# Window and retention scores two heads at a time, modulation chunks in pairs

## The chip, the core and the metric

The kernel runs on one core of a Trainium2 chip. The metric is the time of one execution on the device, in microseconds (us). TensorE is called PE here, its weight loads PEld, VectorE DVE, ScalarE ACT, GpSimd POOL and SyncE SP.

## What is computed

One inference step of a two-layer diffusion transformer, for 128 context tokens (block 0) and 256 latent tokens (blocks 1 and 2) of 1024 elements. Layer 0 mixes by retention (8 heads) beside banded attention (8 query heads, 2 key heads, 64 elements each); layer 1 by differential attention beside a Fourier transform; each layer ends in a SwiGLU network. Shift, scale and gate of each layer come from a conditioning vector. What matters here, cut from the reference:

```python
mod = jax.nn.silu(cond) @ w_mod[l] + b_mod[l]
sh1, sc1, g1, sh2, sc2, g2 = jnp.split(mod[:, None, :], 6, axis=-1)
u = layer_norm(x) * (1.0 + sc1) + sh1
...
band = jnp.abs(a - b + Q_BLOCK) <= WINDOW
s = jnp.einsum('bqhgd,bkhd->bhgqk', q, k).astype(f32) * (q.shape[-1] ** -0.5)
s = jnp.where(mask, s, -jnp.inf)
p = jax.nn.softmax(jnp.concatenate([s, sink_col], -1), axis=-1)[..., :-1]
return jnp.einsum('bhgqk,bkhd->bqhgd', p.astype(v.dtype), v)
...
att = jnp.einsum('bhid,bhjd->bhij', qc, kc) * intra
o = jnp.einsum('bhij,bhjv->bhiv', att, vc) + jnp.einsum('bhid,bhdv->bhiv', qc, s) * q_decay[..., None]
```

## The kernel before

Python code names every instruction; a scheduler puts those of each engine into one order by priority and by its own estimate of when they are ready, and each engine's queue then runs in that order. `hmm` (L116) issues a product with raised priority. Tiles come from pools with a fixed number of buffers: a new tile of a name's tag waits until an old one has been read for the last time.

Large weights are read as 512 KB units into `raw` tiles (`raw_unit`, L157, five buffers), and `split` (L167) makes two tiles of each, the rounded value (ACT, a cast into tag `wr`) and the remainder (DVE, a subtraction into tag `wl`); each tag has five buffers (`NWR`, L41). A `raw` buffer is free after the split. A block of 128 tokens against a slab of 512 columns is 24 products of 512 columns, 3 per 128 rows of the model dimension (`in_block`, L366), into a bank of PSUM from `bankA` (L82), of which there are two.

The stretch of the change is `mixer_ab`, layer 0. Its steps stand in `AORDER` (L33): a letter and a number each, in the order in which the code issues them. `Q`, `G` load the slabs `rqk` and `rvg` of a half of the retention heads (half 0 is heads 0 to 3, half 1 heads 4 to 7), `R`, `V` multiply them, `W` advances the window, `C` does the retention of a half (`ret_core`, L1037), `N` its norm, `M` one modulation vector of layer 0 (2 the gate, 3 the shift, 4 the scale), `E` loads the units `wo` of the output projection. The loads are issued by SP in program order.

The window goes head by head: `win1` (L846) makes the scores `ws` of one head (64 rows of the array, the upper or the lower by the head's parity), adds the mask with a product of `ident` and `wm` in fp32, takes the maximum on DVE and the exponentials on ACT; `win2` (L869) normalizes, transposes 128 columns at a time (`tw`) and multiplies by the values (`wpo`: 64 columns of the array, again by parity). `win1` runs `WDEPTH` = 3 heads ahead (L892), in three banks `S`; `tw` and `wpo` have one bank each (`pto`, L1326). An fp32 product that is no transpose is two instructions in the profile.

A modulation vector (`mod_pe`, L218) is 8 chunks of 512 KB that pass through the `raw` tiles with no split: four products per chunk, each on 32 columns of the array, all added up in the one bank `M` (`Banks("pab", S=3, M=1)`, L829), which nothing else uses. The gate's row then goes to DRAM over SP's queue (`gs`, `mod_scratch`, L276), 8 small transfers.

Of the kernel before, what the change touches and what calls it, by code (L numbers as in the profile page):

```python
# [32 lines left out]
AORDER = "Q0 R0 W8 T G0 D V0 M0 Q1 W24 M1 G1 C0 E M2 N1 R1 N2 V1 C1 X N0 N4 N3 N5"  # L33
# [31 lines left out]
def trunk_kernel(ctx: ExitStack, tc: tile.TileContext, a: dict):  # L65
# [19 lines left out]
    class Banks:  # L85
# [60 lines left out]
    # biases of the shifts and scales as columns: (layer, vector, chunk), the scales' with one added  # L146
# [84 lines left out]

    def mod_steps(l, v, out):
# [18 lines left out]
        # keep cond 0 in row 32*j, cond 1 in row 32*j + 1  # L251
# [78 lines left out]
    def ln_chain(b, x, s, sums, lnv, name, junk, fast=False, final=False):  # L330
        """both layer norms of a block in stages; yields after each"""
# [83 lines left out]
    def run_order(order, steps):  # L415
        """steps by their letters, with the number that follows"""
# [245 lines left out]
    def start_phase(u, ap, pto):  # L662
        """modulation, first u and the first two slabs of layer 0, a step of the model dimension at a time"""
# [12 lines left out]
        # a step is one or two chunks of 128 elements of the shift and the scale; condition c of its product lies in row  # L676
        # 32*(2*scale + j) + c, where j counts the chunks, or the halves of the sum where there is but one chunk
# [135 lines left out]
    def mixer_ab(u, cat, early, early_es, ap, ap_es, pto, mt, gm, wkT, wv, wqT, mods):  # L813
# [15 lines left out]
        bk = Banks("pab", S=3, M=1)  # L829
# [3 lines left out]
        if True:  # L833
            sink = ap2.tile([P, 2, HEADS], F32, name="sink")
            SY.dma_start(sink[:, 0, :], bc(a["win_sink"][0:1, :]))
            wm = ap2.tile([P, 2, P], F32, name="wm")
# [7 lines left out]
            wst = {}  # L844

            def win1(b, h):  # L846
                nk = 1 if b == 0 else 3
                w = nk * P
                k0 = 0 if b == 0 else P
                c, q, kv = h // 2, h % 2, h // 4  # L850
                rows = slice(64 * q, 64 * q + 64)
# [11 lines left out]
                S.activation(pt[:, 0:w], ps[:, 0:w], AF.Exp, bias=nm, scale=0.125, accum_out=sm)
                S.activation(es, sink[:, 0, h : h + 1], AF.Exp, bias=nm)
                wst[b, h] = (pt, es, sm)

            wpo = {}

            def win2(b, h):  # L869
# [3 lines left out]
                c, q, kv = h // 2, h % 2, h // 4  # L873
                pt, es, sm = wst.pop((b, h))
                V.tensor_tensor(sm, sm, es, ALU.add)
                V.reciprocal(sm, sm)
                V.tensor_scalar(pt[:, 0:w], pt[:, 0:w], sm, None, ALU.mult)
                pT = ap2.tile([P, 3, P], F32, tag="pT", name=f"wpT{b}_{h}", bufs=5)
                transpose_to(pT[:, 0:nk, :], [pt[:, i * P : (i + 1) * P] for i in range(nk)], pto("T", f"tw{b}_{h}"))
                if q == 0:  # L880
                    wpo[0] = pto("O", f"wpo{b}_{c}")
                po = wpo[0]
# [3 lines left out]
                if q == 1:  # L886
                    cat_split(cat, 4 + c, 1, slice(b * P, (b + 1) * P), po[:, 0:P])

            items = [(b, h) for b in range(NB) for h in range(HEADS)]
# [70 lines left out]
            def sc_sample(hh, q):  # L960
                qk = half[hh][0]
                c, par = q // 2, q % 2
                rows = slice(64 * par, 64 * par + 64)
                at = ap2.tile([P, 2, 256], F32, tag="pT", name=f"at{hh}_{q}", bufs=5)
                ps = bk("S", f"rs{hh}_{q}")
                for ji in range(2):
                    hmm(ps[:, ji * 256 : ji * 256 + 256], qk[rows, 2 + c, (1 + ji) * P : (2 + ji) * P],
                        qk[rows, c, P:NTOK], start=True, stop=True)
                for ji in range(2):
                    V.scalar_tensor_tensor(at[:, ji, :], ps[:, ji * 256 : ji * 256 + 256], 0.125,  # L970
                                           mt[hh][:, q, P - P * ji : P - P * ji + 256], ALU.mult, ALU.mult)
                return at
# [112 lines left out]
            def end_ab():  # L1085
# [5 lines left out]
                               "D": load_rest, "E": end_early, "X": end_ab, "M": lambda i: mods[i](bk)})  # L1091
# [233 lines left out]
    for l in range(2):  # L1325
# [9 lines left out]
        if l == 0:  # L1335
            def mod_ab(v, bk):
# [165 lines left out]
```

## Time and profile before

| what | value |
|---|---|
| median of 3 runs | 1034.05 us (1032.87 to 1034.13) |
| span of the profiled execution, first to last instruction | 1032.0 us |
| PE, DVE, ACT busy | 98%, 62%, 42% of the span |
| PE's mean granted clock | 0.997 |
| moved by DMA | 172.86 MB, 168 GB/s |

The span is that of one profiled execution; the time of an execution as the runs give it holds the span and what lies around it. Busy time counts an engine's instructions; a matmul's end is modelled, and the durations of successive ones overlap, so the start of the next is the better measure of a price. "wg" and "wu" are the feed-forward network's products, "dn" its down projection: they fill most of the span, after 240 us.

### The profile page before, as it was taken

What the parts mean: (1) busy time and instruction counts of PE and PEld (TensorE: products, weight loads), DVE (VectorE), ACT (ScalarE), POOL (GpSimd) and SP (SyncE); (2) the same over time, 40 slices, a digit from 0 to 9 for tenths busy, and PEclk for the clock granted to TensorE, in tenths of its full rate; (3) what the DMA queues carried; (4) which work ended last, traced back from release to release, by engine and by line L of the source; (5) the groups of instructions that cost most, each with busy time, mean ns of one, the idle gap of its engine ahead of it and who ended that gap; (6) DMA issues with size and microseconds to landing.
All of it is one profiled execution on the core that took longest, in us unless ns stands there. A gap on an engine that the chain in (4) does not pass through costs nothing.

```text
span 1032.0 us, 14970 instructions
## 1 busy us (share of the span) xinstructions
PE 1010.3 (98%) x5695; PEld 840.5 (81%) x5695; DVE 639.7 (62%) x1390; ACT 437.4 (42%) x798; POOL 1.2 (0%) x5
## 2 busy tenths in 40 slices
PE   9999999999999999999999999999999999999996
PEld 4775667687899999989987766687889999999985
DVE  5477637768794968769648477638853333334544
ACT  3385524234743243233527655634843333333410
POOL 0000000000000000000000000000000000000000
PEclk9999999999999999999999999999999999999998
DMA  9975254763687767665724332126375333343401
GB/s 299 293 200 204 63 163 141 257 195 120 214 302 235 241 206 228 222 216 185 243 82 161 104 93 92 68 91 245 123 268 170 127 130 123 123 123 123 164 21 41
DMA packets 109704, 172.86 MB, mean 168 GB/s; under 512 B 10176, under 2 KB 78272, under 8 KB 109632
## 3 DMA queue, kind: packets, MB, share of 16 engines
q1 hardware_dynamic: 106960, 170.87, 50.7%
q10 hardware_dynamic: 2672, 1.04, 0.4%
q8 instruction: 45, 0.74, 0.3%
q14 instruction: 27, 0.22, 0.1%
HBM read 167.52 MB, written 4.36 MB: 167 GB/s over the span
## 4 chain that ended last, share of the span: by engine, by line
PE 85%; DVE 6%; DMA 5%; ACT 2%; issue 1%; SPq 0%; ACTq 0%; DVEq 0%
PE dn L513 16%; PE wg L537 15%; PE wu L537 14%; PE cd L372 8%; PE wo L372 5%; PE rvg L372 3%; PE s L372 3%; PE rqk L372 2%; PE ws L114 2%; PE ds L114 2%; PE wpo L114 2%; PE hg L372 2%; PE hu L372 1%; PE mod L114 1%; PE ms L114 1%
## 5 line engine op out<-in xcount | busy, mean ns | idle before, releaser
L537 PE MATMUL wg<-urf,r_wg 128*128 128x384 f32 x320 | 108.2, 340 | 1.8 <-DVE sg L554 1.8
L537 PE MATMUL wg<-ulf,r_wg 128*128 128x384 f32 x320 | 108.5, 339 | 0.0
L537 PE MATMUL wu<-ulf,r_wu 128*128 128x384 f32 x320 | 108.3, 338 | 0.0
L537 PE MATMUL wu<-urf,r_wu 128*128 128x384 f32 x320 | 108.1, 339 | 0.0
L537 PE MATMUL wg<-urf,l_wg 128*128 128x384 f32 x320 | 108.1, 338 | 0.0
L537 PE MATMUL wu<-urf,l_wu 128*128 128x384 f32 x320 | 108.1, 338 | 0.0
L244 DVE SCALAR_TENSOR_TENSOR z<-mraw,cs,z 128x1024 f32<-128x1024 f32 x70 | 86.1, 1280 | 12.9 <-DMA mraw<-in_w_mod 12.8
L170 DVE TENSOR_TENSOR l_wg<-raw_wg,r_wg 128x1024 fp32r<-128x1024 f32 x40 | 48.7, 1223 | 66.9 <-ACT r_wg L168 66.8
L170 DVE TENSOR_TENSOR l_wd<-raw_wd,r_wd 128x1024 fp32r<-128x1024 f32 x36 | 44.0, 1223 | 52.8 <-ACT r_wd L168 52.7
L168 ACT CAST r_wd<-raw_wd 128x1024 fp32r<-128x1024 f32 x36 | 37.8, 1050 | 86.0 <-PE wu L537 38.8
L170 DVE TENSOR_TENSOR l_wu<-raw_wu,r_wu 128x1024 fp32r<-128x1024 f32 x40 | 48.6, 1222 | 39.3 <-ACT r_wu L168 39.3
L168 ACT CAST r_wg<-raw_wg 128x1024 fp32r<-128x1024 f32 x40 | 42.0, 1049 | 72.0 <-PE dn L513 29.9
L168 ACT CAST r_wu<-raw_wu 128x1024 fp32r<-128x1024 f32 x40 | 42.0, 1050 | 60.7 <-PE wu L537 20.4
L513 PE MATMUL dn<-r_wd,hr 128*128 128x512 f32 x168 | 66.6, 396 | 0.0
L513 PE MATMUL dn<-l_wd,hr 128*128 128x512 f32 x168 | 66.6, 396 | 0.0
L513 PE MATMUL dn<-r_wd,hl 128*128 128x512 f32 x168 | 66.5, 396 | 0.0
L537 PEld LDWEIGHTS wg<-urf,r_wg 128*128 128x128 f32 x320 | 60.1, 188 | 4.4 <-DVE sg L554 2.9
L537 PEld LDWEIGHTS wu<-urf,r_wu 128*128 128x128 f32 x320 | 60.1, 188 | 1.7 <-ACT r_wg L168 0.8
L537 PEld LDWEIGHTS wu<-ulf,r_wu 128*128 128x128 f32 x320 | 60.1, 188 | 0.5
L537 PEld LDWEIGHTS wg<-ulf,r_wg 128*128 128x128 f32 x320 | 60.1, 188 | 0.5
L537 PEld LDWEIGHTS wg<-urf,l_wg 128*128 128x128 f32 x320 | 60.1, 188 | 0.0
L537 PEld LDWEIGHTS wu<-urf,l_wu 128*128 128x128 f32 x320 | 60.1, 188 | 0.0
(415 smaller groups left out, 2220.2 us busy)
## 6 DMA issues: line engine op xcount, KB each, us to landing
raw_wd<-in_w_down SPq DMA_DIRECT2D x44, 512.0 KB
rawm<-in_w_mod SPq DMA_DIRECT2D x40, 512.0 KB
mraw<-in_w_mod SPq DMA_DIRECT2D x40, 512.0 KB
raw_wg<-in_w_gate SPq DMA_DIRECT2D x40, 512.0 KB
raw_wu<-in_w_up SPq DMA_DIRECT2D x40, 512.0 KB
raw_cd<-in_w_in_cd SPq DMA_DIRECT2D x20, 512.0 KB
ms<-in_w_mod SPq DMA_DIRECT2D x16, 512.0 KB
raw_rqk<-in_w_in_ab SPq DMA_DIRECT2D x16, 256.0 KB
```

Source lines behind the costliest of these rows:

```text
L114: return f(*args, **kw)
L168: S.copy(r, t)
L170: V.tensor_tensor(lo, t, r, ALU.subtract)
L244: V.scalar_tensor_tensor(z[c], t, cs[:, c, k : k + 1], z[c], ALU.mult, ALU.add)
L372: op = mm(ps[:, col : col + width], u[pu][:, k0 + kk, b * P : (b + 1) * P], (r, lo)[pw][:, kk, :], start=(first and i == 0 and pu + pw == ...
L513: mm(acc[b, nh], h[fc][ph][:, b * P : (b + 1) * P], wrl[pw][:, nh * 512 : (nh + 1) * 512], start=(fc == 0 and ph + pw == 0), stop=(last an ...
L537: mm(ps[j][:, 0:NTOK], un[i][pw][:, k, j * P : (j + 1) * P], u2[pu][:, 4 * i + k, :], start=(i == 0 and k == 0 and pu + pw == 0), stop=(i ...
```

## The change

The window takes two heads (a pair) at a time: scores of both into a pair of banks, the mask added by a two-byte (BF16) product each, one reduction, one exponential of both sinks; the values' products alternate between the heads. There are two pairs `S`, and `WDEPTH` counts pairs. The retention scores take pairs too. The bank `M` is gone: a modulation vector is made in four batches of two chunks, each batch in a bank of `bankA`, and added up on DVE; the later chunk of a batch is multiplied first. Lines are those of the files before and after.

```diff
-AORDER = "Q0 R0 W8 T G0 D V0 M0 Q1 W24 M1 G1 C0 E M2 N1 R1 N2 V1 C1 X N0 N4 N3 N5"
+AORDER = "Q0 R0 W4 T G0 D V0 M0 Q1 W12 M1 G1 C0 E M2 N1 R1 N2 V1 C1 X N0 N4 N3 N5"
...
+MBATCH = 2
-WDEPTH = 3
+WDEPTH = 2
...
+        def pair(self, tag, name):
+            return self.pool.tile([P, 2, 512], F32, tag=tag, name=name, bufs=self.tags[tag])
...
+    def mod_batches(l, v):
+        w = a["w_mod"][l].rearrange("(p k) n -> p k n", k=KC)
+        bm = mod_tile(l, v)
+        for k0 in range(0, KC, MBATCH):
+            ts = [raw_unit(w[:, k, v * D : (v + 1) * D], [D], f"rawm{l}_{v}_{k}") for k in range(k0, k0 + MBATCH)]
+            ps = bankA(f"mod{l}_{v}_{k0}")
+            order = [MBATCH - 1] + list(range(MBATCH - 1))
+            for n, i in enumerate(order):
+                for j in range(4):
+                    hmm(ps[32 * j : 32 * j + 32, 0:256], cmod[:, k0 + i, :], ts[i][:, j * 256 : (j + 1) * 256],
+                        start=(n == 0), stop=(n == MBATCH - 1))
+            if k0 > 0 or v in (2, 5):
+                V.tensor_tensor(bm, ps[:, 0:256], bm, ALU.add)
+            else:
+                V.tensor_copy(bm, ps[:, 0:256])
+        return bm
...
-        bk = Banks("pab", S=3, M=1)
+        bk = Banks("pab", S=2)
...
-            wm = ap2.tile([P, 2, P], F32, name="wm")
+            wm = mid([P, 2, P], "wm")
...
+            identb = ap2.tile([P, P], BF16, name="identb")
+            V.tensor_copy(identb, ident)
+            wmb = ap2.tile([P, 2, P], BF16, name="wmb")
+            V.tensor_copy(wmb, wm)
...
-            def win1(b, h):
+            def win1(b, c):
...
-                ps = bk("S", f"ws{b}_{h}")
-                hmm(ps[:, 0:w], wqT[rows, c, b * P : (b + 1) * P], wkT[rows, kv, k0 : k0 + w], start=True, stop=(b == 0))
+                ps = bk.pair("S", f"ws{b}_{c}")
+                for q in range(2):
+                    rows = slice(64 * q, 64 * q + 64)
+                    hmm(ps[:, q, 0:w], wqT[rows, c, b * P : (b + 1) * P], wkT[rows, kv, k0 : k0 + w], start=True, stop=(b == 0))
...
-                    hmm(ps[:, mc * P : (mc + 1) * P], ident, wm[:, b - 1, :], start=False, stop=True)
+                    for q in range(2):
+                        hmm(ps[:, q, mc * P : (mc + 1) * P], identb, wmb[:, b - 1, :], start=False, stop=True)
...
+                V.reduce_max(nm, ps[:, :, 0:w], AX.X)
+                V.scalar_tensor_tensor(nm, nm, -0.125, sink[:, 1, hs], ALU.mult, ALU.min)
+                V.tensor_tensor(es, nm, sink[:, 0, hs], ALU.add)
...
+                S.activation(es, es, AF.Exp)
...
                 for i in range(nk):
-                    hmm(po[64 * q : 64 * q + 64, 0:P], wv[:, tiles[i], kv * 64 : kv * 64 + 64], pT[:, i, :],
-                        start=(i == 0), stop=(i == nk - 1))
+                    for q in range(2):
+                        hmm(po[64 * q : 64 * q + 64, 0:P], wv[:, tiles[i], kv * 64 : kv * 64 + 64], pTs[q][:, i, :],
+                            start=(i == 0), stop=(i == nk - 1))
...
-                ps = bk("S", f"rs{hh}_{q}")
+                ps = bk.pair("S", f"rs{hh}_{c}")
                 for ji in range(2):
+                    for par in range(2):
+                        rows = slice(64 * par, 64 * par + 64)
...
-                mp = mod_pe(0, v, bk("M", f"mod0_{v}"))
+                mp = mod_batches(0, v)
...
-                    m[0, v] = mod_cols(mp, 0, v, bk("M", f"modt0_{v}"))
+                    m[0, v] = mod_cols(mp, 0, v, bankA(f"modt0_{v}"))
```

What stands where in the queues, at three places. First PE in the window's block 2 (`ws_` and `wpo_` are followed by the head before, by the pair in the change; in the change `tw_1_1` is pair 1, its second head; a row is one product, or as many as its x says). Before:

```order
L114 MATMUL ws_2_1543<-wkT,wqT 128x384
L114 MATMUL wpo_2_1465<-wpT_5_1483,wv 64x128 x3
L114 MATMUL tw_6_1509<-ident,wp_6_1453 128x128 x3
L114 MATMUL ws_2_1543<-wm,ident 128x128
L114 MATMUL ws_3_1567<-wkT,wqT 128x384
L114 MATMUL wpo_3_1514<-wpT_6_1508,wv 64x128 x3
L114 MATMUL tw_7_1533<-ident,wp_7_1477 128x128 x3
L114 MATMUL ws_3_1567<-wm,ident 128x128
```

One head after the other: its scores, three products and three transposes of earlier heads, its mask. In the change:

```order
L119 MATMUL ws_0_1442<-wkT,wqT 128x384
L119 MATMUL tw_1_1_1387<-ident,wp_1_1_1332 128x128 x3
L119 MATMUL wpo_1_1392<-wpT_1_0_1379,wv 64x128
L119 MATMUL ws_0_1442<-wkT,wqT 128x384
L119 MATMUL wpo_1_1392<-wpT_1_1_1386,wv 64x128
L119 MATMUL wpo_1_1392<-wpT_1_0_1379,wv 64x128
L119 MATMUL wpo_1_1392<-wpT_1_1_1386,wv 64x128
L119 MATMUL wpo_1_1392<-wpT_1_0_1379,wv 64x128
L119 MATMUL wpo_1_1392<-wpT_1_1_1386,wv 64x128
L119 MATMUL tw_2_0_1421<-ident,wp_2_0_1371 128x128 x3
```

The two score products of a pair have a head's transposes and one product with the values between them; the other five products with the values follow each other, by turns of the two heads.

Second, PE where half 1's first slab `rqk` begins (`mod_4` is vector 4, `rawm_4_5` its chunk 5, `rot` a transpose of the norm, `modt` the column product). Before, chunks of vector 4 stand between products of `rqk`:

```order
L372 MATMUL rqk_1_2028<-r_rqk_3_1343,ul_91 128x512
L372 MATMUL rqk_1_2028<-l_rqk_3_1344,ur_90 128x512
L372 MATMUL rqk_2_2065<-r_rqk_0_1322,ur_90 128x512
L114 MATMUL mod_4_1903<-rawm_4_1_1911,cmod 32x256 x4
L372 MATMUL rqk_2_2065<-r_rqk_0_1322,ul_91 128x512
L372 MATMUL rqk_2_2065<-l_rqk_0_1323,ur_90 128x512
L372 MATMUL rqk_2_2065<-r_rqk_0_1322,ur_90 128x512
L372 MATMUL rqk_2_2065<-r_rqk_0_1322,ul_91 128x512
L114 MATMUL mod_4_1903<-rawm_4_2_1917,cmod 32x256 x4
```

Some products of the slab lie between one chunk and the next. In the change (`rawm_4_1` is again vector 4's chunk 1):

```order
L119 MATMUL mod_3_6_1678<-rawm_3_6_1674,cmod 32x256 x4
L119 MATMUL modt_3_1688<-sel,bm_3_1631 128x8 x2
L119 MATMUL mod_4_0_1825<-rawm_4_1_1823,cmod 32x256 x4
L119 MATMUL mod_4_0_1825<-rawm_4_0_1821,cmod 32x256 x4
L119 MATMUL mod_4_2_1839<-rawm_4_3_1837,cmod 32x256 x4
L119 MATMUL mod_4_2_1839<-rawm_4_2_1835,cmod 32x256 x4
L119 MATMUL mod_4_4_1853<-rawm_4_5_1851,cmod 32x256 x4
L119 MATMUL mod_4_4_1853<-rawm_4_4_1849,cmod 32x256 x4
L119 MATMUL mod_4_6_1867<-rawm_4_7_1865,cmod 32x256 x4
L119 MATMUL mod_4_6_1867<-rawm_4_6_1863,cmod 32x256 x4
L119 MATMUL modt_4_1877<-sel,bm_4_1820 128x8 x2
L395 MATMUL rqk_0_1922<-r_rqk_0_1294,ur_90 128x512
```

The last row is the first product of `rqk` 1: all batches of vectors 3 and 4 stand ahead of it now. Before, all 72 of its products stood ahead of vector 4's last chunk. The four batches of vector 2 stand among the products of `rvg` 0's last block in the change, the first of them behind five of its 24 products; behind that block come `po`, `st`, and then vector 3, with a transpose or two of the norm between its batches.

Third, SP's queue at the same place of the program, in the change (`raw_rqk` is half 1's; x2 are the two halves of a unit):

```order
L845 DMA raw_rqk_0_1291<-in_w_in_ab 128x2x256 x2
L845 DMA raw_rqk_1_1298<-in_w_in_ab 128x2x256 x2
L845 DMA raw_rqk_2_1305<-in_w_in_ab 128x2x256
L303 DMA gs_2_1282<-bm_2_1221 1x256 x8
L845 DMA raw_rqk_2_1305<-in_w_in_ab 128x2x256
L845 DMA raw_rqk_3_1312<-in_w_in_ab 128x2x256 x2
L164 DMA rawm_3_0_1632<-in_w_mod 128x1024
L164 DMA rawm_3_1_1634<-in_w_mod 128x1024
```

Before, the same rows stand there, except that the 8 `gs` came one row later, behind both halves of `raw_rqk_2`. In both, 8 chunks of vector 3, the four units `raw_rvg`, three of `raw_wo` and 8 chunks of vector 4 follow in this order.

## Rows read from the trace of the kernel before

**Rows 1.** The page, parts 1 and 4: busy time, and the chain by engine:
```profile
span 1032.0 us, 14970 instructions
...
PE 1010.3 (98%) x5695; PEld 840.5 (81%) x5695; DVE 639.7 (62%) x1390; ACT 437.4 (42%) x798; POOL 1.2 (0%) x5
...
PE 85%; DVE 6%; DMA 5%; ACT 2%; issue 1%; SPq 0%; ACTq 0%; DVEq 0%
```

**Rows 2.** PE's timeline, one head: start us, us, line, instruction:
```profile
111.18 0.91 PE L114 MATMUL ws<-wkT,wqT 64*128 64x384 f32 x2
112.02 0.87 PE L114 MATMUL wpo<-wpT,wv 128*64 128x128 f32 x6
112.81 0.55 PE L114 MATMUL tw<-ident,wp 128*128 128x128 f32 x3
113.20 0.39 PE L114 MATMUL ws<-wm,ident 128*128 128x128 f32 x2
113.52 0.91 PE L114 MATMUL ws<-wkT,wqT 64*128 64x384 f32 x2
```

**Rows 3.** Stretches: length, PE, PEld, DVE, ACT, POOL busy us, PEclk, DMA share, GB/s:
```profile
120.00:130.00 10.00, 10.00 (x58) 6.53 (x58) 5.91 (x23) 5.64 (x19) 0.00 (x0) 1.00 0.01 2
```

**Rows 4.** Stretches of tile `rs` alone: length, PE, PEld, DVE busy us, PEclk, DMA, GB/s:
```profile
136.53:137.59 1.06, 1.06 (x4) 0.67 (x4) 0.00 (x0) 1.00 0.05 19
141.21:143.13 1.92, 1.92 (x12) 1.45 (x12) 0.76 (x3) 1.00 0.77 222
```

**Rows 5.** The same of `mod` alone; then of slab `rvg` alone, with ACT's column:
```profile
131.72:132.72 1.00, 1.00 (x14) 0.40 (x14) 0.00 (x0) 1.00 0.00 0
145.15:146.07 0.92, 0.57 (x8) 0.16 (x8) 0.00 (x0) 1.00 0.87 214
...
152.54:156.48 3.94, 3.94 (x18) 3.20 (x17) 0.00 (x0) 0.26 (x1) 1.00 0.37 122
```

**Rows 6.** PE around half 1's start: timeline; then `po`'s busy time in a stretch:
```profile
161.87 0.39 PE L372 MATMUL rqk<-r_rqk,ur 128*128 128x512 f32 x1
...
177.64 0.64 PE L114 MATMUL mod<-rawm,cmod 128*32 128x256 f32 x8 [0.74 <-DMA rawm<-in_w_mod]
...
161.87:172.60 10.73, 4.95 (x42) 4.86 (x42) 0.84 (x2) 0.74 (x2) 1.00 0.60 187
```

**Rows 7.** SyncE's queue: start us, us, loads issued:
```profile
72.27 22.52 SPq L159 DMA_DIRECT2D rawm<-in_w_mod  x8
...
103.16 2.36 SPq L280 DMA_DIRECT2D gs<-bm  x8
...
132.40 0.81 SPq L159 DMA_DIRECT2D rawm<-in_w_mod  x2
139.57 0.33 SPq L159 DMA_DIRECT2D rawm<-in_w_mod  x1
...
172.47 16.88 SPq L159 DMA_DIRECT2D rawm<-in_w_mod  x8
```

**Rows 8.** Stretches, as above: DMA traffic around two loads, and at its highest:
```profile
6.00:8.00 2.00, 2.00 (x6) 0.71 (x4) 1.78 (x6) 0.00 (x0) 0.00 (x0) 1.00 1.01 384
190.00:195.00 5.00, 4.25 (x32) 2.14 (x34) 3.94 (x7) 0.47 (x1) 0.00 (x0) 1.00 0.98 364
...
133.00:136.50 3.50, 3.50 (x26) 2.43 (x25) 0.79 (x4) 0.86 (x3) 0.00 (x0) 1.00 0.85 294
...
140.50:142.25 1.75, 1.75 (x17) 1.12 (x16) 0.29 (x1) 0.27 (x1) 0.00 (x0) 1.00 0.87 295
```

**Rows 9.** Stretches, as above: PE's clock over a wait and after the last product:
```profile
176.00:178.00 2.00, 1.26 (x12) 0.53 (x10) 1.95 (x8) 0.85 (x3) 0.00 (x0) 1.00 0.37 110
...
1026.00:1028.00 2.00, 0.00 (x0) 0.00 (x0) 1.82 (x10) 0.14 (x2) 0.00 (x0) 0.50 0.00 0
```

**Rows 10.** Groups of instructions, 60 to 220 us: busy us, mean ns | idle before:
```profile
L170 DVE TENSOR_TENSOR l_rvg<-raw_rvg,r_rvg 128x1024 fp32r<-128x1024 f32 x8 | 9.7, 1218 | 1.1 <-ACT r_rvg L168 1.0
...
L168 ACT CAST r_rvg<-raw_rvg 128x1024 fp32r<-128x1024 f32 x8 | 8.4, 1054 | 9.5 <-PE rqk L372 9.1 <-PE rvg L372 0.3
```

More of the change, by code (lines that the diff above doesn't have):

```diff
@@ L863, in win1 @@
[L863 to L869, printed above, removed]
+                    for q in range(2):
+                        hmm(ps[:, q, mc * P : (mc + 1) * P], identb, wmb[:, b - 1, :], start=False, stop=True)
+                nm = small([P, 2], "wnm")
+                es = small([P, 2], "wes")
@@ new lines, in win1 @@
+                sm = small([P, 2], "wsm")
+                V.reduce_max(nm, ps[:, :, 0:w], AX.X)
+                V.scalar_tensor_tensor(nm, nm, -0.125, sink[:, 1, hs], ALU.mult, ALU.min)
+                V.tensor_tensor(es, nm, sink[:, 0, hs], ALU.add)
+                pts = []
+                for q in range(2):
+                    pt = early.tile([P, 384], F32, tag="p", name=f"wp{b}_{c}_{q}", bufs=4)
+                    S.activation(pt[:, 0:w], ps[:, q, 0:w], AF.Exp, bias=nm[:, q : q + 1], scale=0.125,
+                                 accum_out=sm[:, q : q + 1])
+                    pts.append(pt)
@@ L870, in win2 @@
+                S.activation(es, es, AF.Exp)
+                wst[b, c] = (pts, es, sm)
+            def win2(b, c):
                 nk = 1 if b == 0 else 3
@@ L872, in win2 @@
                 tiles = [0] if b == 0 else [1, 2, 3]
[L873 to L874 removed]
+                kv = c // 2
+                pts, es, sm = wst.pop((b, c))
                 V.tensor_tensor(sm, sm, es, ALU.add)
                 V.reciprocal(sm, sm)
[L877 to L882, printed above, removed]
[L883 to L889 removed]
+                pTs = []
+                for q, pt in enumerate(pts):
+                    V.tensor_scalar(pt[:, 0:w], pt[:, 0:w], sm[:, q : q + 1], None, ALU.mult)
+                    pT = ap2.tile([P, 3, P], F32, tag="pT", name=f"wpT{b}_{c}_{q}", bufs=5)
+                    transpose_to(pT[:, 0:nk, :], [pt[:, i * P : (i + 1) * P] for i in range(nk)], pto("T", f"tw{b}_{c}_{q}"))
+                    pTs.append(pT)
+                po = pto("O", f"wpo{b}_{c}")
+                for i in range(nk):
+                    for q in range(2):
+                        hmm(po[64 * q : 64 * q + 64, 0:P], wv[:, tiles[i], kv * 64 : kv * 64 + 64], pTs[q][:, i, :],
+                            start=(i == 0), stop=(i == nk - 1))
+                cat_split(cat, 4 + c, 1, slice(b * P, (b + 1) * P), po[:, 0:P])
+            items = [(b, c) for b in range(NB) for c in range(4)]
             state = {"n1": 0, "n2": 0}
@@ L948, in sc_prompt @@
                 at = ap2.tile([P, 2, 2, P], F32, tag="pT", name=f"atp{hh}", bufs=5)
-                pss = [bk("S", f"rsp{hh}_{par}") for par in range(2)]
+                pp = bk.pair("S", f"rsp{hh}")
+                pss = [pp[:, par, :] for par in range(2)]
                 for c in range(2):
@@ L958, in sc_prompt, with sc_sample @@
                 return at
-            def sc_sample(hh, q):
+            def sc_sample(hh, c):
                 qk = half[hh][0]
-                c, par = q // 2, q % 2
-                rows = slice(64 * par, 64 * par + 64)
-                at = ap2.tile([P, 2, 256], F32, tag="pT", name=f"at{hh}_{q}", bufs=5)
-                ps = bk("S", f"rs{hh}_{q}")
+                ps = bk.pair("S", f"rs{hh}_{c}")
                 for ji in range(2):
[L967 to L972, printed above, removed]
+                    for par in range(2):
+                        rows = slice(64 * par, 64 * par + 64)
+                        hmm(ps[:, par, ji * 256 : ji * 256 + 256], qk[rows, 2 + c, (1 + ji) * P : (2 + ji) * P],
+                            qk[rows, c, P:NTOK], start=True, stop=True)
+                ats = []
+                for par in range(2):
+                    at = ap2.tile([P, 2, 256], F32, tag="pT", name=f"at{hh}_{c}_{par}", bufs=5)
+                    for ji in range(2):
+                        V.scalar_tensor_tensor(at[:, ji, :], ps[:, par, ji * 256 : ji * 256 + 256], 0.125,
+                                               mt[hh][:, 2 * c + par, P - P * ji : P - P * ji + 256], ALU.mult, ALU.mult)
+                    ats.append(at)
+                return ats
             def ret_out(hh, b, po):
@@ L1038, in ret_core @@
                 ap_ = sc_prompt(hh)
-                ats = [sc_sample(hh, q) for q in range(4)]
+                ats = sc_sample(hh, 0) + sc_sample(hh, 1)
                 r0 = av_prompt(hh, ap_)
@@ L1340, in mod_ab @@
                 else:
-                    m[0, v] = mod_cols(mp, 0, v, bk("M", f"modt0_{v}"))
-            pre, wxr_es = mixer_ab(u, cat, early, early_es, ap1, ap1_es, pto, *first, [lambda bk, v=v: mod_ab(v, bk) for v in (2, 3, 4)])
+                    m[0, v] = mod_cols(mp, 0, v, bankA(f"modt0_{v}"))
+            pre, wxr_es = mixer_ab(u, cat, early, early_es, ap1, ap1_es, pto, *first, [lambda v=v: mod_ab(v) for v in (2, 3, 4)])
         else:
```

17 lines of the change are left out of this document (5 added, 12 removed).

## The prediction

> **What bounds the kernel now.** I read the page first [rows 1]: PE is busy 98% of the span and holds 85% of the chain that ended last, so a microsecond taken from PE's queue is a microsecond of the kernel, and a wait put into that queue is one too, unless it takes the place of another. Then the window's stretch on PE [rows 2]: one head of a latent block is a run of scores (`ws`), output products (`wpo`), transposes (`tw`) and mask product (`ws<-wm`), and from one `ws` to the next it is 113.52 - 111.18 = 2.34 us, without a gap. ACT and DVE have slack there, 5.64 and 5.91 of 10 us [rows 3]. Then the modulation chunks: in this kernel they lie between other products, so PE waits for their loads only twice, 0.74 and 0.75 us [rows 6], although SyncE's queue brings them in slowly, as buffers come free [rows 7]. The reader is to see in these groups that the products are cheap and that the loads are covered by other products.
>
> **The change, part by part.**
>
> *Window products.* Heads 0 to 7 of blocks 1 and 2 make 16 of the 2.34 us cycles. What halves side by side bring is seen for the retention scores, where heads alternate between rows 0-63 and 64-127: one head takes 1.06 us for 4 instructions, 0.265 each, three heads 1.92 us for 12, 0.16 each [rows 4], 0.6 of it. In the order of the change the two `ws` of a pair are mostly parted by `tw` and a `wpo`, so I count no gain for them. The `wpo` of a pair alternate by column half: 2 x 0.80 us [rows 2] for six products, 0.27 us each, become one single product of 0.27 and five in alternation at 0.6 of that, 1.07 us. The mask product loses half of its two passes, 0.32 us becoming about 0.17 us. That is 0.53 + 0.3 = 0.83 us per pair, 8 pairs, and 0.9 taken for block 0's four: **-7.5 us**. Ends: -3 us if halves gain nothing and only the mask's second pass goes (16 x 0.2), -16.6 us if every `ws` and `wpo` ran at half its time (16 x 0.82) and the mask saved 0.22 each. ACT's and DVE's slack covers the wider reduction and the pair's exponentials; if it did not, a pair would wait part of a microsecond, which the end of -3 holds.
>
> The Trainium skill (TensorEngine Tiling (Array Packing), Key Properties) says that tiles work independently, which would give that end of -16.6 and a sum 9 us lower; the same section says that a change of tiling mode drains the array, and here whole-array transposes lie between the halves, so I stay with the rows.
>
> *Retention scores of the second half*, now four alternating products in a row, twice: 1.92 + 1.06 us for 16 instructions become 2.56 at 0.16 each and 2.1 at half of 0.265; I take the second, since every product has its partner beside it: **-0.9 us** (ends 0 and -1.5).
>
> *Modulation batches.* A chunk costs 0.92 - 0.23 = 0.69 us of PE between other products (0.92 us is a chunk and one product of 0.232), 24 of them 16.6 us; 14 instructions in a row took 1.00 us, so 16 take 1.15 us [rows 5], and 12 batches 13.8 us: **-3 us** (ends 0 and -4.7). The two old waits go as well: **-1.5 us**.
>
> *What is moved.* This decides. All 12 batches now take a bank of `bankA`, of which there are two, and which the slabs `rqk` and `rvg` use. In program order vector 2 comes behind `rvg` 0, and `rqk` 1 behind vectors 3 and 4; in the order, PE has the first batch of vector 2 five products into the last block of `rvg` 0, and not one product of `rqk` 1 before the last batch of vector 4. The loads are held back with it: `raw` has 5 buffers, five chunks of vector 2 sit in them from about 75 us on, and everything behind them in SyncE's queue waits for PE to consume them. Between the first batch of vector 2 and the first product of `rqk` 1, 30 loads of 512 KB (3 of vector 2, 4 `rqk`, 8 of vector 3, 4 `rvg`, 3 `wo`, 8 of vector 4) must go through the queue in turn, and PE's own work there is small: 19 `rvg` products x 0.232 = 4.4 us, 11 batches x 1.15 = 12.7, `po` and `st` 5.8 (4.95 [rows 6], and an estimate of 0.8 for four small products), small transposes some 1.5: 24.4 us.
>
> Price of a load: of the pair issued at 132.40, 1.05 MB, 294 GB/s x 3.5 us = 1.03 MB had moved by 136.5, so a pair lands 4.1 us behind its issue; of the one issued at 139.57, 0.52 MB, 295 x 1.75 = 0.52 MB had by 142.25, 2.7 us [rows 7, 8]. A split is a cast of 1.05 and a subtraction of 1.22 us, 2.3 us in all [rows 10]. From the end of vector 2's first batch, in us:
> - chunks 5 and 6 land at 4.1; third batch done at 5.2; ten `rvg` products; fourth batch done at 8.7.
> - The copy to DRAM (`gs`) stands in SyncE's queue ahead of three `rqk` halves and vector 3: it waits for vector 2's last sum on DVE, and its 8 issues take 2.36, the three halves some 1.2 (two issues take 0.81 [rows 7]). Vector 3's first pair is issued at 13, behind 0.8 MB of `rqk`, and lands at about 19; PE has done `po` and `st` by 15. First batch done at 20.
> - three more batches, whose pairs overlap in part with one another (buffers come free from the `rqk` splits): 3.3 each, done at 30.
> - the `rvg` loads fill three buffers for good, since their splits need `wr` tiles that `rqk` 1 has not released. `wo` and vector 4 pass through the two others: a load, a split, the next load, its split, 13 us up to the issue of vector 4's second chunk at 43.
> - vector 4: one chunk 2.7 + 1.15, then three round trips of 4.1 + 1.15, and 0.5 for the column product: `rqk` 1 starts at 63.
>
> So PE has 63 us for 24.4 us of work: **+39 us** of waits. Bounds: the highest rate in the rows is 384 GB/s [rows 8], at which 30 x 0.524 MB take 41 us, so at least 17 us of waits; and if no pair overlapped with another, 11 x 5.3 + 16 + 5 = 79 us, 55 us of waits. Behind these waits in PE's queue stand `rqk` 1, `rvg` 1 and the whole rest, and ACT and DVE have nothing to do meanwhile; nothing later is late in the kernel before (PE is saturated), so nothing gives it back.
>
> *The clock.* PE's clock stayed at 1.00 over the wait of 0.74 us in 176-178, but at the end of the span, where PE has nothing to do in 1026-1028, it read 0.50, the level of 1.2 GHz [rows 9]. The new waits of 3 to 4 us with 1.15 us of work between them lie between these two cases, nearer the second: some of the last 8 batches take twice as long and `rqk` 1 begins at half speed. I take **+4 us**, ends 0 and 10.
>
> The Trainium skill (TensorE: Matmul & The Clock Gate, HAM oscillation) describes a kernel whose work between load waits is shorter than the wait, and which finds the clock lowered each time. By that all 8 batches would pay, +9 us and some for `rqk`, 1070 in all; the trace of before has no such pattern.
>
> Sum: -7.5 - 0.9 - 3 - 1.5 + 39 + 4 = **+30 us**. The trace's span is 1032.0 us; the three runs have a median of 1034.05, so about 2 us lie outside the span, which I keep: 1034 + 30 = **1064 us**.
>
> **Rivals.**
> - *Not slower:* the loads run at the highest rate without a gap, the clock stays up and the halves run fully side by side: -16.6 - 1.5 - 3 - 1.5 + 17 = -6, 1028 us. It decides if PE's waits between the two places stay under some 20 us. For it: the queue does reach 364 GB/s for 5 us once several loads are out [rows 8]. Against it: the buffers allow two loads at a time for vector 4, and `gs` stops the queue once.
> - *Shorter wait:* the pairs overlap better, vector 3 is there when PE comes and `wo` costs 8 instead of 13 us: 25 us of waits and no change of clock, +12, 1046 us (1036 to 1050).
> - *Longer wait:* every batch pays a whole round trip (vector 4's first load took 177.64 - 172.47 = 5.2 us from issue to use in the trace [rows 6, 7]) and the clock stays down: -3 - 3 - 1.5 + 55 + 10 = +57, 1091 us (from 1078).
> - *The halves gain nothing, or all they can:* the forecast with -3 or -16.6 for -7.5, 1069 or 1055 us; both lie within the forecast's band and have their chance there.
>
> **How the numbers follow.** Forecast, 1050 to 1078: 0.67. Shorter wait 0.15, longer 0.11, not slower 0.07, of which I give 0.03 to faster by over 0.2% (2 us, about what a measurement of this kernel tells from no change) and 0.03 to no change. Slower: 0.94. The range reaches a little into both neighbours, 1045 to 1080, and leaves out about 2 in 10.
>
> **What would show it.** Right: PE's busy share falls by 3 to 4 points; one stretch of some 60 us, from about 140 to 200, where PE is below half busy, its wait put down to DMA `rawm`; there groups of 16 `mod` instructions stand 4 to 6 us apart, the last four nearest to 5 us, with the clock's row below 1.00; the first product of `rqk` 1 near 200 instead of 161.87; before it, a window pair of about 3.8 us instead of 4.68. Wrong: if PE waits under 20 us there, if the window's cycle stays at 2.34 per head or falls to 1.4, or if waits of the same size turn up in the window itself, on ACT or on the two pairs of banks.

## The result, and the profile after

The change takes 1069.61 us (median of 4 runs, 1069.08 to 1069.93) against 1034.09 us of the kernel before in the same comparison: 1.0336 times as long, with a 95% interval from 1.0319 to 1.0353. That is 35.5 us more, where +30 (1064 us) was forecast and 1045 to 1080 given as the range. The profiled execution has a span of 1068.1 us, 36.1 more than that of [rows 1]. All times below leave out three slow executions that stood far off the others of their kernel (2540 us of `mods_only`, 1092 of `o6`, 1971 of `so8`); the trace kept of `o6` is of its slow one and is not read here.

The page of the change, part 1:

```profile
span 1068.1 us, 14912 instructions
...
PE 1009.9 (95%) x5679; PEld 838.4 (78%) x5679; DVE 639.8 (60%) x1365; ACT 434.3 (41%) x786; POOL 1.2 (0%) x5
```

PE's busy time is the same as before (1009.9 against 1010.3 us), though not its work: as shown further on, the products that the change saves and the time lost to a lower clock cancel out in it. What is new on the page is the time in which PE has nothing to do. Where that lies, the stretches show (columns as in [rows 3]):

```profile
120.00:140.00 20.00, 20.00 (x132) 13.77 (x128) 6.45 (x21) 5.16 (x17) 0.00 (x0) 1.00 0.00 1
140.00:160.00 20.00, 13.78 (x116) 10.07 (x114) 10.51 (x43) 5.76 (x9) 0.00 (x0) 0.95 0.80 263
160.00:180.00 20.00, 10.68 (x74) 4.25 (x74) 11.81 (x50) 2.96 (x5) 0.00 (x0) 0.50 0.90 295
180.00:200.00 20.00, 3.87 (x32) 1.36 (x32) 4.53 (x5) 2.33 (x3) 0.00 (x0) 0.50 0.48 145
200.00:220.00 20.00, 11.30 (x52) 7.39 (x53) 1.09 (x4) 0.00 (x0) 0.00 (x0) 0.51 0.43 152
220.00:240.00 20.00, 20.00 (x98) 16.02 (x97) 10.23 (x16) 6.29 (x8) 0.00 (x0) 1.00 0.26 84
```

One stretch of 80 us, from 140 to 220, holds both losses: PE is busy for 40 of the 80, and from 158 on its clock stands at 0.50, the lower level. On either side of it PE is busy throughout. What ended PE's waits between 60 and 260 us (us in total, times, the longest):

```profile
PE mod L119 <- DMA rawm<-in_w_mod: 30.0, 6, 16.1
PE rot L119 <- DVE ro L1037: 4.7, 2, 3.9
PE rot L119 <- DVE r1ret L195: 2.8, 1, 2.8
PE modt L119 <- DVE bm L250: 1.1, 2, 0.5
...
```

PE's timeline through the stretch (columns as in [rows 2], with the wait before and what ended it in brackets):

```profile
138.40 1.07 PE L119 MATMUL mod<-rawm,cmod 128*32 128x256 f32 x16
...
160.23 0.69 PE L119 MATMUL rot<-ident,ro 128*128 128x128 f32 x2 [3.92 <-DVE ro L1037]
160.85 1.93 PE L119 MATMUL mod<-rawm,cmod 128*32 128x256 f32 x16
165.54 0.45 PE L119 MATMUL rot<-ident,ro 128*128 128x128 f32 x1 [2.76 <-DVE r1ret L195]
...
173.94 1.02 PE L119 MATMUL modt<-sel,bm 128*128 128x8 f32 x4 [0.55 <-DVE bm L250]
191.01 1.94 PE L119 MATMUL mod<-rawm,cmod 128*32 128x256 f32 x16 [16.05 <-DMA rawm<-in_w_mod]
197.10 1.93 PE L119 MATMUL mod<-rawm,cmod 128*32 128x256 f32 x16 [4.16 <-DMA rawm<-in_w_mod]
203.05 1.94 PE L119 MATMUL mod<-rawm,cmod 128*32 128x256 f32 x16 [4.01 <-DMA rawm<-in_w_mod]
210.10 1.94 PE L119 MATMUL mod<-rawm,cmod 128*32 128x256 f32 x16 [5.12 <-DMA rawm<-in_w_mod]
...
213.45 0.77 PE L395 MATMUL rqk<-r_rqk,ur 128*128 128x512 f32 x1
```

Vector 2's four batches (138.40 to 148.24) still have products between them. Vector 3's stand among transposes `rot`, which wait for the norm on DVE. Vector 4's wait for their loads, 16.05 us and then 4 to 5 us each. `rqk` 1 begins at 213.45; before, at 161.87 [rows 6]. SyncE's queue at the same time:

```profile
152.75 14.63 SPq L164 DMA_DIRECT2D rawm<-in_w_mod  x8
167.91 5.57 SPq L845 DMA_DIRECT2D raw_rvg<-in_w_in_ab  x8
173.57 8.32 SPq L164 DMA_DIRECT2D raw_wo<-in_w_out_ab  x3
183.08 22.28 SPq L164 DMA_DIRECT2D rawm<-in_w_mod  x8
```

Vector 4's first load is issued at 183.08, behind four `rvg` units and three of `wo`; its eight issues take 22 us, since most of them need a buffer that a batch has to free.

The gains are there too. PE's timeline of one pair in the window:

```profile
106.18 0.91 PE L119 MATMUL ws<-wkT,wqT 64*128 64x384 f32 x2
107.02 0.55 PE L119 MATMUL tw<-ident,wp 128*128 128x128 f32 x3
107.49 0.43 PE L119 MATMUL wpo<-wpT,wv 128*64 128x128 f32 x2
107.86 0.91 PE L119 MATMUL ws<-wkT,wqT 64*128 64x384 f32 x2
108.69 0.87 PE L119 MATMUL wpo<-wpT,wv 128*64 128x128 f32 x10
109.50 0.55 PE L119 MATMUL tw<-ident,wp 128*128 128x128 f32 x3
109.88 0.28 PE L119 MATMUL ws<-wmb,identb 128*128 128x128 bf16 x2
110.08 0.91 PE L119 MATMUL ws<-wkT,wqT 64*128 64x384 f32 x2
```

From `ws` to `ws` of the next pair it is 3.90 us, for two heads that took 4.68 [rows 2]. The products with the values take 0.37 + 0.81 = 1.18 us instead of 1.60, the two mask products 0.20 instead of 0.64; each `ws` still takes 0.84.

### The profile page after: what moved, and what is told of

Same layout as the page of the kernel before. It is cut to its first block, busy times and chain, and to the rows that moved or that the text cites. A ratio compares the mean times of both kernels' runs of the same rounds, so it can differ in the third digit from the quotient of the medians.

```text
span 1068.1 us, 14912 instructions
## 1 busy us (share of the span) xinstructions
PE 1009.9 (95%) x5679; PEld 838.4 (78%) x5679; DVE 639.8 (60%) x1365; ACT 434.3 (41%) x786; POOL 1.2 (0%) x5
## 4 chain that ended last, share of the span: by engine, by line
PE 88%; DMA 4%; DVE 4%; ACT 2%; issue 1%; SPq 0%; ACTq 0%; DVEq 0%
PE dn L536 16%; PE wu L560 16%; PE wg L560 16%; PE cd L395 8%; PE wo L395 5%; PE rqk L395 3%; PE rvg L395 3%; PE s L395 2%; DMA rawm<-in_w_mod 2%; PE ds L119 2%; PE hg L395 1%; PE hu L395 1%; PE mod L119 1%; PE ws L119 1%; PE ms L119 1%; PE wpo L119 1%
```

## The experiments

The theory going in: the loss is where the batches stand in PE's order and what their loads pass through, and the window's part is a gain. Rivals: the pairs themselves cost, or the loads are too slow wherever they stand.

**The batches alone** (`mods_only`: the kernel before, with the change's `mod_batches`; window and scores head by head):

```diff
-        bk = Banks("pab", S=3, M=1)
+        bk = Banks("pab", S=3)
...
-                mp = mod_pe(0, v, bk("M", f"mod0_{v}"))
+                mp = mod_batches(0, v)
...
-                    m[0, v] = mod_cols(mp, 0, v, bk("M", f"modt0_{v}"))
+                    m[0, v] = mod_cols(mp, 0, v, bankA(f"modt0_{v}"))
```

> The kernel before with the modulation batches in bankA alone; window and retention scores head by head as before. If the whole loss comes from the batches (their place in PE's order and their loads), this kernel loses it without the window's gain: the pair cycle went from 4.68 to 3.90 us, 8 x 0.78 = 6.2 and about 0.9 for block 0, retention scores 1.0, so 1069.6 + 8 = 1078 us (1074 to 1082). Rival: the pairs, with two pairs of banks for three single ones, carry a part of the loss: then 1069 or less.

Measured: 1078.61 us (median of three), 1.0422 of before (1.0398 to 1.0447). The batches carry the whole loss, 44 us, and the pairs take 9 of it back (1078.61 - 1069.61).

**Vector 4's loads earlier in SyncE's queue** (`m2_early`), PE's order up to `rqk` 1 as it was:

```diff
-... W12 M1 G1 C0 E M2 N1 R1 ...
+... W12 M1 M2 G1 C0 E N1 R1 ...
```

> The change with step M2 (vector 4) ahead of G1 and E in AORDER, so that SyncE loads vector 4 straight behind vector 3, ahead of the slab rvg 1 and of wo; PE's order up to rqk 1 stays the same. If the wait of 16.05 us before vector 4's first batch is the queue's (rvg fills three buffers, wo passes through the others), it falls under 5 us: 1057 to 1061 us, with 5 buffers also shorter waits between the batches. Rival: it is the plain rate of the loads, or PE's order, that costs: within 3 us of 1069.6.

Measured: 1044.58 us, 1.0096 (1.0074 to 1.0118), 25 us below the change, twice what was expected. PE's timeline of vector 4 in this kernel:

```profile
173.75 1.94 PE L119 MATMUL mod<-rawm,cmod 128*32 128x256 f32 x16
176.34 1.55 PE L119 MATMUL mod<-rawm,cmod 128*32 128x256 f32 x16 [0.66 <-DMA rawm<-in_w_mod]
179.95 1.17 PE L119 MATMUL mod<-rawm,cmod 128*32 128x256 f32 x16 [2.05 <-DMA rawm<-in_w_mod]
182.57 1.93 PE L119 MATMUL mod<-rawm,cmod 128*32 128x256 f32 x16 [1.45 <-DMA rawm<-in_w_mod]
```

and SyncE's queue, which has vectors 3 and 4 in a row:

```profile
151.47 26.34 SPq L164 DMA_DIRECT2D rawm<-in_w_mod  x16
```

The four waits were 16.05 + 4.16 + 4.01 + 5.12 = 29.3 us in the change and are 0 + 0.66 + 2.05 + 1.45 = 4.2 here: 25 us, nearly the whole difference (26.4 between the two spans). The expectation had put a price only on the first of them. With all five buffers the loads also follow one another closely: sixteen issues take 26 us where vector 4's eight took 22 through two buffers. So the position of eight loads in SyncE's queue, with PE's order unchanged, is worth most of the loss. The 10 us that are left are mostly not loads: 7.0 us of waits before `rot` stay, and 21.9 us of PE's work between 157 and 191 us are still done at half speed.

**Vector 4 behind `rqk` 1 in PE's order** (`m2_late`), SyncE's queue as it was:

```diff
-... C0 E M2 N1 R1 N2 ...
+... C0 E N1 R1 M2 N2 ...
```

> The change with step M2 behind R1 in AORDER: PE has rqk 1 ahead of vector 4's batches, SyncE's queue stays in its order (rvg 1, wo, vector 4). If the place in PE's order decides, rqk 1's 17 us cover the queue, the wait of 16.05 us goes and most of the three of 4 to 5: 38.5 us of the stretch become some 9, 1040 us (1033 to 1046). Rival: vector 4's loads still pass through two buffers while rqk 1 holds the weights of rvg 1, and the waits turn up behind rqk 1: 1055 us or more.

Measured: 1044.87 us, 1.0096 (1.0075 to 1.0116). The same gain by the other way: `rqk` 1 covers the queue. What is left of the waits in the trace is 6.2 us for `rawm` and 6.7 for `rot`. Either is enough; it took both together to cost 25 us.

**All three vectors ahead of `rvg` 0** (`o6`), among the window's products:

```diff
-AORDER = "Q0 R0 W4 T G0 D V0 M0 Q1 W12 M1 G1 C0 E M2 N1 R1 N2 V1 C1 X N0 N4 N3 N5"
+AORDER = "Q0 R0 W4 T G0 D M0 M1 M2 V0 Q1 W12 G1 C0 E N1 R1 N2 V1 C1 X N0 N4 N3 N5"
```

> The change with all three M steps ahead of V0 in AORDER: vectors 2, 3 and 4 are loaded (12.6 MB) and multiplied among the window's products, rvg 0 behind the window. If order and queue were the whole loss, what is left is the gain: window 7.1, retention scores 1.0, batches 4.1, old waits 1.5 = 13.7, 1020 us (1016 to 1026). Rival: the 24 loads do not come in fast enough within the window's 45 us, or without rvg 0 as filler the pairs wait for ACT and DVE: over 1030 us.

Measured: 0.9956 of before (0.9932 to 0.998), about 1030 us: some 5 us faster than the kernel before, 10 above the expectation, and on the border of the rival. Where those 10 us lie is not shown for this order; the next one keeps vector 2 in the same place.

**Each vector in a place of its own** (2 ahead of `rvg` 0, 3 in the last block of `rvg` 0, 4 in that of `rvg` 1), with pairs (`o8`) and then head by head (`so8`, which is `mods_only` with these steps, `W8` and `W24` as its window counts heads):

```diff
-AORDER = "Q0 R0 W4 T G0 D V0 M0 Q1 W12 M1 G1 C0 E M2 N1 R1 N2 V1 C1 X N0 N4 N3 N5"
+AORDER = "Q0 R0 W4 T G0 D M0 V0 M1 Q1 W12 G1 C0 E N1 R1 N2 V1 M2 C1 X N0 N4 N3 N5"
```

> The change with M0 ahead of V0, M1 behind V0, and M2 behind V1 in AORDER: vector 2 is multiplied among the window's products, vector 3 in the last block of rvg 0, vector 4 in the last block of rvg 1, and rqk 1 follows rvg 0 directly. If the loss is only where the batches stand and what their loads wait for, all of it goes and the gains stay: window 7.1, retention scores 1.0, batches 4.1, old waits 1.5 = 13.7 off 1034, 1020 us (1017 to 1026). Rival: the batches meet their loads late at the new places as well, or the window waits for ACT and DVE without rvg 0 among its products: 1030 us or more.

> The same step order with the kernel before's window and retention scores, head by head (batches as in the change). It should be slower than the pairs in the same order by their gain alone: 6.2 (8 x 0.78) + 0.9 for block 0 + 1.0 for the scores = 8 us (6 to 10), so about 1028. Rival: where the loads are covered the pairs bring nothing, ACT or DVE end the window: a difference under 3 us.

Measured: 1028.39 us with pairs, 0.9954 (0.9938 to 0.9969); 1038.54 us head by head, 1.003 (1.0014 to 1.0046). The difference, 10.2 us by the medians and 7.9 by the ratios, is roughly the gain of the pairs, where 6 to 10 were expected; roughly, since both kernels also lose time to the clock, and not the same in each execution. The trace of the kernel with pairs is of the longest of its twelve executions (1025.42 to 1034.2 us). PE's timeline and the clock's row (a stretch as above) show a loss that the expectation did not have:

```profile
93.05 1.07 PE L119 MATMUL mod<-rawm,cmod 128*32 128x256 f32 x16
94.05 0.92 PE L119 MATMUL ws<-wkT,wqT 64*128 64x384 f32 x4
...
97.56 1.07 PE L119 MATMUL mod<-rawm,cmod 128*32 128x256 f32 x16 [2.37 <-DVE wnm L891]
```

```profile
100.00:120.00 20.00, 20.00 (x106) 9.91 (x106) 8.19 (x28) 7.78 (x26) 0.00 (x0) 0.67 0.48 167
```

PE waits 2.37 us for DVE, then 0.62 more, and runs the next 13 us at the lower level: (1 - 0.67) x 20 = 6.6 us lost behind 3 us of waiting. In the change, products of `rvg` 0 stood at this place. The loss by the clock differs from one execution to the next: the granted clock was 0.988 in that of 1034.2 us, 0.992 in those near the median and 0.993 to 0.995 in the five shortest. Against 0.997 in the trace of the kernel before, 0.992 makes some 5 us (an estimate, 0.005 x 1028), so by this the clock is most of the 8 us by which the median lies above 1020.

**The first block of `rvg` 0 put back there** (`h8`), and then vector 3 behind it too, vector 4 behind `rvg` 0 (`h9`):

```diff
+                    if (hh, b) == (0, 0):
+                        mods[0]()
```

in `rvg_slab`, behind a block's evacuation (`h9`: and `mods[1]()`), with the steps (the first line is `h8`, the second `h9`)

```diff
+AORDER = "Q0 R0 W4 T G0 D V0 M1 Q1 W12 G1 C0 E N1 R1 N2 V1 M2 C1 X N0 N4 N3 N5"
+AORDER = "Q0 R0 W4 T G0 D V0 M2 Q1 W12 G1 C0 E N1 R1 N2 V1 C1 X N0 N4 N3 N5"
```

> As o8, but vector 2's batches are issued behind the first block of rvg 0 (so that its 24 products stand among the window's first pairs, ahead of vector 2), vector 3 behind rvg 0, vector 4 behind rvg 1. In o8 PE waited 2.37 us before vector 2's second batch and 0.6 behind it, and the clock's row fell to 0.67 over 100 to 120 us, 6.6 us of work lost. If it was the missing rvg 0 products, both go: 1028.4 - 9 = 1019 us (1017 to 1023), pairs at 3.9 us throughout. Rival: DVE's queue holds that bank whatever stands before, the wait moves: 1026 or more.

> As h8, but vectors 2 and 3 both behind the first block of rvg 0, and vector 4 in vector 3's place behind rvg 0, so that no load of a modulation chunk stands behind rvg 1's in SyncE's queue and the loads of the output phase come earlier. In o8 PE waited 3.6 us for chunks of vector 5 in the output phase, and 0.9 + 0.9 + 0.3 nearby. If those waits come from vector 4's late loads, h9 is 3 to 5 us faster than h8: 1015 us. Rival: 16 chunks do not come in fast enough among the window's products: PE waits there, 1020 or more.

Measured: 1023.65 us, 0.9888 (0.9857 to 0.9919), and 1018.13 us, 0.9824 (0.979 to 0.9858). In `h8` both the wait and the low clock are gone (1.00 over 100 to 120 us), as expected if it was the missing `rvg` 0 products that had opened the wait. The time is just above the expected band: the expectation took the 9 us of `o8`'s longest execution off `o8`'s median, which held less of them (from one trace to the other it is 11.6 us, 1034.2 to 1022.61). The waits in the output phase stayed, 2.4 us for vector 5's chunks and 2.1 around them. In `h9` these are gone as well, and it is 5.5 us faster, where 3 to 5 were expected. All 24 chunks are multiplied between other products, at the full clock; the group of their instructions between 60 and 260 us (busy us, mean ns | idle before):

```profile
L119 PE MATMUL mod<-rawm,cmod 128*32 128x256 f32 x192 | 12.8, 385 | 0.5 <-DMA rawm<-in_w_mod 0.4
```

This version has the change's products and batches, and is some 17 us faster than the kernel before, 51 faster than the change.

**The clock** (`busy4`). Products that nobody reads fill vector 4's waits (60 before its first batch, 18 each before the third and fourth):

```diff
+NKEEP = {0: 60, 2: 0, 4: 18, 6: 18}
...
+            if v == 4:
+                for _ in range(NKEEP[k0]):
+                    hmm(ps[:, 0:384], u[0][:, 0, 0:P], u[0][:, 1, 0:384], start=True, stop=True)
```

> The change with products that nobody reads in vector 4's banks ahead of its batches (60 of 384 columns before the first, 18 before the third and 18 before the fourth), so that PE is busy while it waits for the loads. If the lowered clock costs time by itself, the last batches take 1.07 instead of 1.94 us and the 14 slow products of rqk 1 take 0.23 instead of 0.43: 4 x 0.87 + 2.8 + 0.4 = 6.7, 1063 us (1061 to 1066). Rival: the slow batches lie beside loads that end the waits anyway and only the slow rqk products count, 2.8 or less: 1067 or more.

Measured: 1066.06 us, 1.0302 (1.0285 to 1.032), 3.6 us below the change, on the border between the expected band (up to 1066) and the rival (from 1067). PE's timeline:

```profile
172.24 1.02 PE L120 MATMUL modt<-sel,bm 128*128 128x8 f32 x4 [0.53 <-DVE bm L254]
173.11 12.29 PE L120 MATMUL mod<-ur 128*128 128x384 f32 x60
189.62 1.32 PE L120 MATMUL mod<-rawm,cmod 128*32 128x256 f32 x16 [4.22 <-DMA rawm<-in_w_mod]
195.35 1.93 PE L120 MATMUL mod<-rawm,cmod 128*32 128x256 f32 x16 [4.41 <-DMA rawm<-in_w_mod]
197.21 5.46 PE L120 MATMUL mod<-ur 128*128 128x384 f32 x21
202.60 1.07 PE L120 MATMUL mod<-rawm,cmod 128*32 128x256 f32 x16
...
208.33 1.07 PE L120 MATMUL mod<-rawm,cmod 128*32 128x256 f32 x16 [1.85 <-DMA rawm<-in_w_mod]
```

The fill did not reach the end of the first wait and left the second open, so two batches were still slow in part or in whole (1.32 and 1.93 us). Nor are the 3.6 us all the clock's: this kernel was 1.7 us ahead of the change before the first filling product (vector 3's column product starts at 172.24, in the change at 173.94), from places ahead of the fill. From there to `rqk` 1 it takes 38.17 us instead of 39.51, 1.3 less, though the faster batches and vector 4's column product gained 0.62 + 0.87 + 0.87 + 0.4 = 2.8: the rest went into waits for loads and into filling products, which the third batch stood behind. `rqk` 1 then left the low level after some 9 products instead of 14, and its first 14 products take 1.2 us less. So of 4.0 us of faster work some 2.6 came through. Slow clock is a loss of its own here, but a part of it lies beside the loads, as the rival says; how large that part is in the change, without filling products, is not shown.

**The parts of the pair.** The mask in fp32 (`mask32`), and the products with the values not in turns (`noalt`):

```diff
-                        hmm(ps[:, q, mc * P : (mc + 1) * P], identb, wmb[:, b - 1, :], start=False, stop=True)
+                        hmm(ps[:, q, mc * P : (mc + 1) * P], ident, wm[:, b - 1, :], start=False, stop=True)
```

```diff
-                for i in range(nk):
-                    for q in range(2):
+                for q in range(2):
+                    for i in range(nk):
```

> The change with the window's mask product in fp32 as before (ident and wm instead of the BF16 copies), all else as in the change. A pair's two mask products took 0.21 us together in the change and one of fp32 0.32 before: 8 x (0.64 - 0.21) = 3.4 us more, 1073 us. Rival: the mask's passes lie beside other work, and nothing changes: within 1 us of 1069.6.

> The change with the products of the values not in turns: three of the first head, then three of the second. The pair's six products took 0.36 + 0.80 = 1.16 us in turns, 2 x 0.80 before; if it is the turns that hide them, 8 x 0.44 = 3.5 us more, 1073 us, and a pair's cycle of 4.3. Rival: the saving has another cause (fewer, wider steps around them): within 1 us of 1069.6 and a cycle of 3.9.

Measured: 1071.74 us, 1.0362 (1.0343 to 1.0382), and 1071.13 us, 1.0351 (1.0316 to 1.0385). Both lie 1.5 to 2 us above the change, between theory and rival, and their intervals overlap with the change's: by the total neither is settled, the scheduler also put `rqk` and `rvg` products elsewhere in both, and the trace of `mask32` has some 3 us more of slow clock, behind a wait of 2.07 us near 73 us. The timelines settle the prices. With the fp32 mask, a pair's masks from their start to the next product's:

```profile
101.91 0.71 PE L119 MATMUL ws<-wm,ident 128*128 128x128 f32 x4
102.55 0.87 PE L119 MATMUL wpo<-wpT,wv 128*64 128x128 f32 x10
```

0.64 us against 0.20. Without turns, a pair's products with the values and what follows:

```profile
115.62 1.56 PE L119 MATMUL wpo<-wpT,wv 128*64 128x128 f32 x12
117.12 0.55 PE L119 MATMUL tw<-ident,wp 128*128 128x128 f32 x3
```

1.50 us for six products without a break, against 0.37 + 0.81 in turns; a pair's cycle there (first `ws` at 109.96 and at 114.31) is 4.35 us, where 4.3 was expected if the turns matter and 3.9 if not. The turns do hide products, and the two-byte mask does cost a third.

## Why the prediction was right, and where it was not

**The mechanism was right.** The batches moved ahead of `rqk` 1, and their loads could not come in behind one another; this lies where it was put, the kernel with the batches alone shows that nothing else was slower, and moving loads or batches took the loss away. (No run gave the four batches a bank of their own; that the shared banks are what fixes their place is read from the order of the queue.) Of the five signs named, three came: busy share 98 to 95%, one stretch from about 140 on in which PE is half busy, and a pair of 3.90 us (3.8 forecast). Two came in part: the last vector's batches are 6 to 7 us apart, where 4 to 6 was named, with the clock's row at 0.50; and `rqk` 1, named near 200, came at 213.45.

**Term by term.** *Window:* -7.5 forecast, about -8.4 measured: 8 x 0.78 = 6.2, 1.4 for the score products of block 0 (PE busy 3.1 us before, 1.7 after), and 0.8 for one pair whose two `ws` stood together (below). The values' products came at 1.18 where 1.07 was set, the masks at 0.20 where 0.17 was set for a single one: the first gained a little less than thought and the second a little more. The end of -16.6, by which tiles work independently (the Trainium skill, TensorEngine Tiling (Array Packing), Key Properties), was not reached: `ws` kept its 0.84 us where transposes parted its two halves. Where the order did put them together, both took 0.84 us, up to the mask at 96.04:

```profile
95.20 0.92 PE L119 MATMUL ws<-wkT,wqT 64*128 64x384 f32 x4
```

*Retention scores:* `rs` took 6.24 us in all before and 5.23 after, -1.0 against -0.9; eight alternating instructions take 1.07 us, half of 0.265 each. So with partners next to one another the halves do work side by side here. *Batches:* 16.1 us before, 12.8 at the full clock in `h9`: -3.3 against -3.

*Waits:* +39 forecast. From the end of vector 2's first batch to `rqk` 1, PE waited 30.0 us for loads and 10.4 for DVE (7.5 before `rot`, 1.1 before the column products, 1.8 before `po` and `st`), 40.4 in all. The sum was right, its parts less so, and that they agree to 1.4 us is in part luck: the working counted only loads, and had PE reach vector 3's first batch early and wait for the load until 20 us after the first batch of vector 2. In the run it was a transpose of the norm, ahead of the batch in the order, that waited 3.92 us for DVE. With loads moved forward these waits stayed (7.0 us in `m2_early`), with `rqk` 1 directly behind `rvg` 0 only 0.7 us was left, so they belong to PE's order. The wait before vector 4 was worked out well: its first batch ended 53.5 us after that of vector 2 (139.40 to 192.9), by the forecast about 47, and 4 of these 6.5 us were there already when vector 3 ended (34 instead of 30).

*The clock* is the step that failed: +4 forecast with an end of 10. The rows give 12.6. The row of the whole slow stretch:

```profile
158.00:219.40 61.40, 25.25 (x156) 12.55 (x157) 18.96 (x61) 6.82 (x9) 0.00 (x0) 0.50 0.62 204
```

PE did 25.25 us of work at half speed, 12.6 us more than at full speed. The forecast had the clock fall late and for "some of the last 8 batches"; it fell at 158 already, during the wait of 3.92 us for the norm, and with more waits behind that one it did not rise again until `rqk` 1 had run for 6 us without a gap. The Trainium skill (TensorE: Matmul & The Clock Gate, HAM oscillation), quoted for this in the prediction, would have had all 8 batches pay, 1070 us in all. The trace agrees with it in that 8 batches take 1.94 us each, though the first fall came in a wait for DVE and not for a load. The evidence against it was only that the trace of before had no such pattern; with two waits of 0.7 us for its loads, that trace could not have one. As a price of the clock alone 12.6 us is an upper bound: in `busy4` only 2.6 of 4.0 us of faster work came through.

*Sum:* -8.4 - 1.0 - 3.3 - 1.5 + 40.4 + 12.6 = +38.8 up to the output projection, whose first product came 39.0 us later than before (255.7 and 216.7). A wait of 1.6 us for a cache load, which the trace of before has at 64 us, gave way to two on ACT of 1.6 in all. Behind that point PE waited 6.1 us in the trace of before and 3.6 in that after, and 36.1 us were left at the end. The forecast's "nothing gives it back" was off by these 2.5. So the time came out above the forecast by the clock (8.6 more), while each of the other terms is within 2.5 us of its forecast.

**The rivals.** *Not slower* and *shorter wait* both needed the loads to overlap; with two buffers they did not, and with five (`m2_early`) they did. *Longer wait* asked for 55 us of waits and 10 for the clock: its clock came, its waits did not.

## What to carry to other kernels

When an accumulation moves from a bank of its own to shared banks, look at where it comes to stand in the engine's order, and so at when its load buffers come free: read the load queue behind it before counting what the products save. A chain of waits has two handles, the place of the products and the place of the loads; here either one gave back 25 of 35 us, without touching a product. And a wait of a few microseconds with little work behind it is to be priced twice, once as a wait and once as the work behind it at half speed; the second price is an upper bound where that work lies beside further loads.

## What was not expected

A wait of 2.37 us with another of 0.62 close behind cost 6.6 us of clock in the trace of `o8`, twice its own length, in the midst of the window's work; the low level lasted 13 us although PE had no gap in them. The trace of `so8` has the same behind a wait of only 1.40 us for a load (its clock is 0.50 from 96 to 108 us, with PE busy throughout), while the kernel before kept 1.00 over its waits of 0.74 us. And 60 filling products (12.3 us of busy PE) brought the clock back to 1.00 in `busy4` but did not hold it: the batch behind the following wait of 4.22 us became slow in its course, and the one behind a further wait of 4.41 us took 1.93 us. The stretches of that kernel:

```profile
177.00:179.00 2.00, 2.00 (x14) 2.00 (x13) 0.19 (x1) 1.05 (x1) 0.00 (x0) 1.00 0.42 156
...
190.00:192.00 2.00, 0.94 (x16) 0.13 (x4) 0.42 (x1) 0.00 (x0) 0.00 (x0) 0.58 0.40 47
192.00:194.00 2.00, 0.00 (x0) 0.00 (x0) 0.00 (x0) 0.00 (x0) 0.00 (x0) 0.50 0.92 365
```

Here a fill that ended before the wait did bought little for the work behind it: 0.62 us of that batch, for 12.3 us of filling products.
